# One product ahead of Down at the boundaries of the SwiGLU parts, product 3 last, fewer raw tiles at stage entries, and a layer norm in small steps

## The chip, the core and the metric

The kernel runs on one core of a Trainium2 chip. The metric is the device time of one execution in microseconds. The engines are named TensorE (PE; its weight loads are PEld), VectorE (DVE), ScalarE (ACT), GpSimd (POOL) and SyncE (SP); each runs its own queue in order and waits on semaphores of the others.

## The reference, cut to what matters

Two layers; x is 512 tokens by 1024 in float32. Each layer is two SwiGLUs with a mixer between them, each behind an RMS norm:

```
def swiglu(x, w_gate, w_up, w_down):
    return (jax.nn.silu(x @ w_gate) * (x @ w_up)) @ w_down
...
    for layer in range(DEPTH):
        x = x + 0.5 * swiglu(rms_norm(x, ffn_pre_norm[layer]), ffn_pre_w_gate[layer],
                             ffn_pre_w_up[layer], ffn_pre_w_down[layer])
        h = rms_norm(x, mix_norm[layer])
        if layer % 2 == 0:
            ...
            x = x + even_mixer(h, ...)
        else:
            ...
            x = x + odd_mixer(h, ...)
        x = x + 0.5 * swiglu(rms_norm(x, ffn_post_norm[layer]), ...)
    return rms_norm(x, final_norm)
```

The hidden width of a SwiGLU is 2816. The even mixer joins block-sparse attention with a gMLP: `u * (W_s LN(v) + b)` over chunks of 128 tokens, where LN is a layer norm over groups of 64 channels. The odd mixer is differential attention. Both end in an output projection.

## The kernel before, in words

All activations stay in SBUF, transposed: a tile is 128 channels by 512 tokens. Every product in float32 is made of three matmuls on split operands: each operand is rounded to a high part (`w_hi`, `xh`, `h`; the rounded type is called fp32r) and a low part, and hi·hi, lo·hi and hi·lo add up in one PSUM bank. Weights stream from HBM: SP issues the DMA of a raw tile, ScalarE makes `w_hi` from it (L127), VectorE makes `w_lo` by a subtraction (L128), and TensorE uses both. All three kinds of tile come from one pool of 14 buffers, `w4`.

`Stream` (L71 to L159) holds the program as a list of slots, each with the weight items that it needs and a function that emits its matmuls. When a slot is emitted, the items of the next three slots are split, and raw tiles further ahead are loaded, as many as the slot's number `raws` allows to be live. `st.later(n, fn)` puts a function n steps later. A scheduler makes every engine's queue out of these calls; the queues below are read from the built program.

A SwiGLU (`ffn`, L419) has 22 blocks of 128 hidden channels, 11 and their partners 11 further on. Block 0, 1 and their partners are done plainly (`first`, `gate`, `up`); the others in steps s of two partners by a Strassen–Winograd scheme of seven products in place of eight (`Seven`, L343; `Up`, L499). A product of a step is 24 matmuls of 128 by 256. Products 1, 6, 7 and 4 add up in bank A, product 2 in bank B, products 5 and 3 in bank D, and VectorE reads the banks between them:

```
    BANK = {1: "A", 6: "A", 7: "A", 4: "A", 2: "B", 5: "D", 3: "D"}
```

c11 (L543) reads B behind product 2, c22 (L556) reads D behind product 7 and before product 3 may write it, c12 (L566) reads D behind product 3, c21 (L579) reads A behind product 4. Products 5 and 6 take sums of weight quarters, which are made by an accumulating DMA on POOL (L359) and in `z` by VectorE (L369); product 3 takes `z` plus the quarter a12, which a second accumulating DMA loads once more (L384).

The steps are grouped in parts (steps 0 to 2, 3 to 5, 6 to 8, 9 to 10; `PARTS`, L417). The order within a step is 5, 6, 2, 7, product 1 of the next step, 3, 4 (L692). The last step of a part (`last(s)`) makes the operands of Down piecewise as soon as a quarter is there (`late`), so that Down can follow at once. Down multiplies the part's hidden blocks by their share of the down weights, again with seven products (`Down`, L591; 18 matmuls each), and its products stand in a list with the first products of the next part's step (L700): p and q are Down for the lower and upper pairs of output blocks, u the next step, v the one behind it. The last part is multiplied plainly (`down`, L615). Between SwiGLUs stand the mixers; `out_proj` (L709) works in chunks `begin` and `end`, and its `done` adds to x and feeds the norm of the SwiGLU that follows (`feed`, three operations on ScalarE and VectorE for each block). In `evac_gate` (L973) of the even mixer the gate is centred, and `finish_gate` (L994) makes the rsqrt for all four token blocks, scales and splits them at one step.

Of the kernel before, what the change touches and what calls it, by code (L numbers as in the profile page):

```python
# [15 lines left out]
OP = mybir.AluOpType  # L16
AX = mybir.AxisListType

P = 128
# [3 lines left out]
TT = T // P  # L23
# [9 lines left out]
def trunk_kernel(ctx: ExitStack, tc: tile.TileContext, a, out):  # L33
# [29 lines left out]
    class Item:  # L63
# [3 lines left out]
        def __init__(self, loads, raw, pre=None, frees=1, free_pre=0, ahead=0, post=None):  # L67
            self.loads, self.raw, self.pre, self.frees, self.free_pre = loads, raw, pre, frees, free_pre
            self.ahead, self.post = ahead, post
# [273 lines left out]
    class Seven:  # L343


        def __init__(self, n, dma):
            self.n, self.dma = n, dma
            self.raw, self.bank = {}, {}

        def load(self, name, *quarters):  # L350
# [11 lines left out]
        def item(self, c):  # L362
            r = self.raw

            def raw(n):
                return lambda: r[n]

            def add(dst, other):
                return lambda: nc.vector.tensor_add(r[dst], r[dst], r[other])  # L369

            if c == 1:
                return Item([self.load("a11", (0, 0))], raw("a11"), frees=0)
            if c == 2:
                return Item([self.load("a12", (0, 1))] if self.dma else [], raw("a12"))
            if c == 3:
                return Item([], raw("z")) if self.dma else Item([self.load("a12", (0, 1))], raw("z"), add("z", "a12"))
            if c == 4:
                return Item([self.load("a22", (1, 1))], raw("a22"))
            if c == 5:
                return Item([self.load("z", (1, 0), (1, 1))], raw("z"), frees=0, ahead=1)  # L380
            if c == 6:
                def post():
                    dst, s = self.source(r["z"], 0, 1)
                    nc.gpsimd.dma_start(dst, s, accum_op=OP.add)  # L384
                return Item([], raw("z"), add("z", "a11"), frees=0, free_pre=1, post=post if self.dma else None)
            return Item([self.load("c", (0, 0), (1, 0))], raw("c"), ahead=1)

        def slot(self, c):
# [30 lines left out]
    def ffn(which, norm, feed):  # L419
# [23 lines left out]
        def last(s):  # L443
            return any(s == e - 1 for _, e in PARTS)
# [54 lines left out]
        class Up(Seven):  # L499

            def __init__(self, s):
                super().__init__(4, True)
                self.s, self.seven = s, seven(s)
                self.late = last(s) and seven(s)
                self.v = {}
# [8 lines left out]
            def after(self, c):  # L514
                s = self.s
                if c in (1, 6):
                    return [(1, lambda: self.copied(c))]
                if c == 2:
                    return [(1, self.c11)]
                if c == 7:  # L520
                    return [(1, self.c22)]
                if c == 3:
                    if self.late:
                        return [(1, self.c12)]
                    return [(1, self.c12), (2, lambda: hidden(s))] + (
                        [] if self.seven else [(2 if last(s) else 3, lambda: whole_split(s))])
                if c == 4:
                    if self.late:
                        return [(1, self.c21)]
                    return [(1, self.c21), (1 if last(s) else 2, lambda: hidden(s + HF))] + (  # L530
                        [(2, lambda: first_operands(s)), (3, lambda: other_operands(s))] if self.seven
                        else [(1 if last(s) else 3, lambda: whole_split(s + HF))])
                return []

            def copied(self, c):
# [55 lines left out]
        class Down(Seven):  # L591

            def __init__(self, d, s0, s1):
                super().__init__(s1 - s0, False)
                self.d, self.s0, self.cols = d, s0, slice(s0 * P, s1 * P)

            def source(self, t, m, half):
# [54 lines left out]
        def first(wg, wu):  # L652
            norm.finish_soon(1 + int(which == 0))
            pg, pu = bank("pg"), bank("pu")
            for ks in [[k] for k in range(KT)] if which == 0 else (ORDER[:-1], ORDER[-1:]):
                for b, w in ((pg, wg), (pu, wu)):
                    project(b, w, norm, ks)
            for p in range(4):
                norm.whole(p)
            st.later(2 + int(which == 0), lambda: product(0, pg, pu))  # L660
            for p in range(4):
                st.later(1 + p, lambda p=p: norm.sums_for(p))

        def gate(f):
            def fn(w):
# [10 lines left out]
                    st.later(1, norm.last_sums)  # L676
            return fn

        def add(items, fn):
            st.add(items, fn, dense=True, raws=7)  # L680

        add([chunk(gu[0, 0]), chunk(gu[0, 1])], first)
        for f in range(plain):
            for f in (f, f + HF):
                if f > 0:
# [3 lines left out]
        steps[plain].add(1)  # L689
        for s0, s1 in PARTS:  # L690
            for s in range(max(s0, plain), s1):
                for c in (5, 6, 2, 7, 1, 3, 4):  # L692
                    if c == 1:
                        if s + 1 < HF and (s == plain or s > s0):
                            steps[s + 1].add(1)
                    elif s == plain or s > s0 or c in (3, 4):
                        steps[s].add(c)
            if s1 < HF:
                p, q, u, v = Down(0, s0, s1), Down(4, s0, s1), steps[s1], steps[s1 + 1]
                for o, c in ((p, 1), (u, 5), (u, 2), (p, 5), (u, 6), (p, 6), (p, 3), (u, 7), (p, 7), (p, 2),  # L700
                             (q, 1), (p, 4), (q, 5), (q, 6), (q, 3), (q, 7), (q, 2), (v, 1), (q, 4)):
                    o.add(c)
                continue
            cols = slice(s0 * P, s1 * P)
            for ds in [ORDER[:2]] + [(d,) for d in ORDER[2:]]:
                add([chunk(wd[0, d][:, cols], wd[1, d][:, cols]) for d in ds], down(ds, s0, s1))


    def out_proj(w, halves, hi, lo, feed):  # L709
        py = {}  # L710

        def mul(d, ws, ks):
            for k in ks:
                s = slice(((d % 2) * 4 + k % 4) * P, ((d % 2) * 4 + k % 4 + 1) * P)
                mm3(py[d], ws[0][:, s], ws[1][:, s], hi[k], lo[k],
                    k == halves[0][0], k == halves[1][-1])

        def done(d):
            nc.vector.tensor_add(x[d], py[d], x[d])
            feed(d)  # L720

        def begin(p):
            def fn(ws):
                for d in (2 * p, 2 * p + 1):
                    py[d] = bank("py")
                    mul(d, ws, halves[0])
            return fn

        def end(p):
            def fn(ws):  # L730
                for d in (2 * p, 2 * p + 1):
                    mul(d, ws, halves[1])
                    done(d)
            return fn

        def end_early(wa, wb):
            done_ks = {d: [] for d in range(4)}
            for k in halves[1]:
                for d in range(4):
                    if k in hi:  # L740
                        mul(d, (wa, wb)[d // 2], [k])
                        done_ks[d].append(k)
                st.step()
            st.drain()
            for d in range(4):
                mul(d, (wa, wb)[d // 2], [k for k in halves[1] if k not in done_ks[d]])
                done(d)

        st.add([chunk(w[0, 0])], begin(0))
        st.add([chunk(w[1, 0])], begin(1))  # L750
        st.add([chunk(w[2, 0])], begin(2))
        st.add([chunk(w[0, 1]), chunk(w[1, 1])], end_early)
        st.add([chunk(w[2, 1])], end(2), raws=7)
        st.add([chunk(w[3, 0])], begin(3), raws=7)
        st.add([chunk(w[3, 1])], end(3), raws=7)


    mask = const.tile([P, 512], F32, name="mask")
# [167 lines left out]
    def even_mixer(norm, feed):  # L926
# [46 lines left out]
        def evac_gate(b):  # L973
            gv = [two("gv") for _ in range(2)]
            for t in range(TT):
                g = gv[t // 2][:, t % 2]
                nc.scalar.activation(g, b[t], AF.Gelu_apprx_tanh, scale=norm.col[:, t:t + 1])
                cen[t] = g
            for t in range(TT):
                st.later(1 + t // 2, lambda t=t: center(t))  # L980
            st.later(3, finish_gate)

        def center(t):
            g = cen[t]
# [6 lines left out]
            nc.gpsimd.tensor_mul(sq, g, g)  # L991
            nc.vector.tensor_reduce(s2[:, t], by_group(sq), axis=AX.X, op=OP.add)

        def finish_gate():  # L994
            rsqrt(rs.rearrange("p t g -> p (t g)"), s2.rearrange("p t g -> p (t g)"), 1.0 / 64, TT * 8)
            for t in range(TT):
                g = cen[t]
                nc.vector.tensor_tensor(by_group(g), by_group(g),
                                        rs[:, t, :, None].to_broadcast([P, 8, 64]), op=OP.mult)
                split_gate(t)  # L1000

        def split_gate(t):
            gh[t], gl[t] = split(cen[t], "g", "h")
# [362 lines left out]
```

## Time and profile before

| | |
|---|---|
| three runs | 1874.03, 1874.51, 1879.26 us (median 1874.51) |
| the profiled execution | 1874.89 us, its span 1873.2 us |
| mean granted TensorE clock | 0.990 of full speed |
| busy | TensorE 1816.5, VectorE 1552.5, ScalarE 961.3, POOL 256.3 us |
| DMA | 288.25 MB in 153831 packets |

The page gives for each engine the time in which it executed something; idle time is put down to what ended it. A wait of TensorE on the path that sets the end costs its full length, and so does a stretch at a lower clock, which shows in the windows as a granted clock below 1.00. Idle time of the other engines costs nothing by itself. Sums below are made against the profiled execution, 1874.89 us, 0.38 us above the median.

### The profile page before, as it was taken

The numbers are of one execution on the slowest core, as the hardware profiler recorded it, in microseconds if no ns is written. First come the engines' busy times: TensorE is split into PE (matmuls) and PEld (weight loads), VectorE is DVE, ScalarE is ACT, GpSimd is POOL, SyncE is SP. The second block draws the span as 40 slices with busy tenths as digits, with TensorE's granted clock in tenths as the row PEclk, the third lists the DMA queues.
The fourth block names the chain that finished last, engine by engine and source line by source line (L and its number), as shares of the span: only waits on it lengthen the run. The fifth ranks groups of instructions, "written<-read, shape, count | busy, mean of one in ns | idle before, by whom it ended". The sixth has DMA issues, their size and how long they took to land. (4 is left out here: it accounts for less than half of the span.)

```text
span 1873.2 us, 32125 instructions
## 1 busy us (share of the span) xinstructions
PE 1816.5 (97%) x12624; PEld 1694.8 (90%) x12624; DVE 1552.5 (83%) x2515; ACT 961.3 (51%) x1523; POOL 256.3 (14%) x247
## 2 busy tenths in 40 slices
PE   7999999999999999999999999999999999999997
PEld 6999999878878999999899999988898789999996
DVE  7889898867957889897978989888889688888976
ACT  6545454533755545454644545464555454454544
POOL 0121111010410111111011212101111001111110
PEclk9999999999999999999999999999999999999999
DMA  7587877412334787876557878751223246878771
GB/s 225 128 218 178 213 177 190 148 61 75 97 106 113 156 225 162 232 162 172 167 121 183 208 188 205 189 156 57 91 80 91 102 116 141 217 163 217 172 193 61
DMA packets 153831, 288.25 MB, mean 154 GB/s; under 512 B 11840, under 2 KB 63696, under 8 KB 153680
## 3 DMA queue, kind: packets, MB, share of 16 engines
q1 hardware_dynamic: 110640, 209.62, 34.7%
q0 software_dynamic: 42464, 75.54, 24.7%
q8 instruction: 99, 1.62, 0.3%
q10 hardware_dynamic: 576, 1.05, 0.1%
q14 instruction: 52, 0.43, 0.1%
HBM read 277.77 MB, written 2.10 MB: 149 GB/s over the span
## 5 line engine op out<-in xcount | busy, mean ns | idle before, releaser
L127 ACT ACTIVATE w_hi<-w_raw 128x1024 fp32r<-128x1024 f32 (+2 forms) x542 | 517.8, 964 | 486.6 <-DVE w_raw L369 107.5
L128 DVE TENSOR_TENSOR w_lo<-w_raw,w_hi 128x1024 fp32r<-128x1024 f32 (+2 forms) x542 | 600.2, 1108 | 181.0 <-ACT w_hi L127 132.8
L359 POOL DMA_DIRECT2D w_raw<-in_gu x72 | 90.2, 1252 | 710.1 <-DMA w_raw<-in_gu 285.7
L402 PE MATMUL pA<-xt,w_hi 128*128 128x256 f32 x576 | 163.3, 284 | 0.7 <-ACT v L537 0.7
L402 PE MATMUL pA<-h,w_hi 128*128 128x256 f32 x576 | 163.0, 283 | 0.0
L403 PE MATMUL pA<-h,w_hi 128*128 128x256 f32 x576 | 163.0, 283 | 0.0
L404 PE MATMUL pA<-h,w_lo 128*128 128x256 f32 x576 | 163.0, 283 | 0.0
L404 PE MATMUL pA<-xt,w_lo 128*128 128x256 f32 x576 | 163.0, 283 | 0.0
L403 PE MATMUL pA<-xl,w_hi 128*128 128x256 f32 x576 | 163.0, 283 | 0.0
L403 PE MATMUL pA<-xt,w_hi 128*128 128x256 f32 x576 | 163.0, 283 | 0.0
L402 PE MATMUL pA<-xh,w_hi 128*128 128x256 f32 x576 | 163.0, 283 | 0.0
L404 PE MATMUL pA<-xh,w_lo 128*128 128x256 f32 x576 | 162.9, 283 | 0.0
L402 PEld LDWEIGHTS pA<-xt,w_hi 128*128 128x128 f32 x576 | 110.6, 192 | 1.0 <-ACT v L537 0.9
L403 PEld LDWEIGHTS pA<-xl,w_hi 128*128 128x128 f32 x576 | 110.6, 192 | 0.3
L402 PEld LDWEIGHTS pA<-xh,w_hi 128*128 128x128 f32 x576 | 110.6, 192 | 0.2
L402 PEld LDWEIGHTS pA<-h,w_hi 128*128 128x128 f32 x576 | 110.6, 192 | 0.0
L403 PEld LDWEIGHTS pA<-h,w_hi 128*128 128x128 f32 x576 | 110.6, 192 | 0.0
L404 PEld LDWEIGHTS pA<-h,w_lo 128*128 128x128 f32 x576 | 110.6, 192 | 0.0
L403 PEld LDWEIGHTS pA<-xt,w_hi 128*128 128x128 f32 x576 | 110.6, 192 | 0.0
L404 PEld LDWEIGHTS pA<-xh,w_lo 128*128 128x128 f32 x576 | 110.6, 192 | 0.0
L404 PEld LDWEIGHTS pA<-xt,w_lo 128*128 128x128 f32 x576 | 110.6, 192 | 0.0
L402 PE MATMUL pD<-h,w_hi 128*128 128x256 f32 x288 | 82.7, 287 | 9.9 <-ACT w_hi L127 9.9
(279 smaller groups left out, 5418.4 us busy)
## 6 DMA issues: line engine op xcount, KB each, us to landing
w_raw<-in_gu SPq DMA_DIRECT2D x210, 512.0 KB, 4.4
w_raw<-in_gu POOLq DMA_DIRECT2D x108, 512.0 KB, 6.1
w_raw<-in_wd SPq DMA_DIRECT2D x120, 384.0 KB, 3.6
w_raw<-in_wd POOLq DMA_DIRECT2D x48, 384.0 KB, 5.7
w_raw<-in_wd SPq DMA_DIRECT2D x64, 128.0 KB, 3.0
w_raw<-in_oqk SPq DMA_DIRECT2D x16, 512.0 KB, 4.6
ks<-ks SPq DMA_DIRECT2D x24, 256.0 KB, 3.4
w_raw<-in_eqk SPq DMA_DIRECT2D x8, 512.0 KB, 3.3
```

The source lines that it names most:

```text
L127: nc.scalar.activation(hi, raw, AF.Copy)
L128: nc.vector.tensor_sub(lo, raw, hi.bitcast(F32))
L359: nc.gpsimd.dma_start(dst, src, accum_op=OP.add)
L402: nc.tensor.matmul(o, w[0][:, s], t[0], start=new and p + j == 0, stop=False, **go)
L403: nc.tensor.matmul(o, w[0][:, s], t[1], start=False, stop=False, **go)
L404: nc.tensor.matmul(o, w[1][:, s], t[0], start=False, stop=p == self.n - 1, **go)
```

## The change

It has five parts. (1) At the boundary of two parts, product 6 of the next step stands ahead of Down's product 5. (2) In steps that are not the last of a part, product 4 stands ahead of product 3, and the work that followed product 4 follows product 3. In the last steps the order stays 3, 4, and `z` gets a12 there by an addition on VectorE, from a raw tile of a12 that is kept, in place of the accumulating DMA (16 of these DMAs fall away). (3) Fewer raw tiles may be live in the first slot of a SwiGLU (5, not 7) and in the last three of an output projection (4, 4 and 5, not 7). (4) In `first`, the sums of the norm's inputs come one step later. (5) In the gMLP's layer norm the rsqrt stands alone at its step, and the four token blocks are scaled and split at the two steps behind it, two at each.

```diff
@@ class Seven, item @@
             if c == 2:
-                return Item([self.load("a12", (0, 1))] if self.dma else [], raw("a12"))
+                known = self.order > 1
+                return Item([] if known else [self.load("a12", (0, 1))], raw("a12"), frees=int(known or self.order == 0))
             if c == 3:
-                return Item([], raw("z")) if self.dma else Item([self.load("a12", (0, 1))], raw("z"), add("z", "a12"))
+                if self.order == 0:
+                    return Item([], raw("z"))
+                known = self.order == 1
+                return Item([] if known else [self.load("a12", (0, 1))], raw("z"), add("z", "a12"), free_pre=int(known))
...
-                return Item([], raw("z"), add("z", "a11"), frees=0, free_pre=1, post=post if self.dma else None)
+                return Item([], raw("z"), add("z", "a11"), frees=0, free_pre=1, post=post if self.order == 0 else None)
@@ class Up, __init__ and after @@
-                super().__init__(4, True)
+                super().__init__(4, int(last(s)))
...
                 if c == 3:
                     if self.late:
                         return [(1, self.c12)]
+                    if last(s):
+                        return [(1, self.c12), (2, lambda: hidden(s)), (2, lambda: whole_split(s))]
                     return [(1, self.c12), (2, lambda: hidden(s))] + (
-                        [] if self.seven else [(2 if last(s) else 3, lambda: whole_split(s))])
+                        [(2, lambda: first_operands(s)), (3, lambda: other_operands(s))] if self.seven
+                        else [(3, lambda: whole_split(s))])
...
@@ class Down, __init__ @@
-                super().__init__(s1 - s0, False)
+                super().__init__(s1 - s0, 2)
@@ ffn @@
             for p in range(4):
-                st.later(1 + p, lambda p=p: norm.sums_for(p))
+                st.later(2 + p, lambda p=p: norm.sums_for(p))
...
-        add([chunk(gu[0, 0]), chunk(gu[0, 1])], first)
+        add([chunk(gu[0, 0]), chunk(gu[0, 1])], first, 5)
...
-                for c in (5, 6, 2, 7, 1, 3, 4):
+                for c in (5, 6, 2, 7, 1, 3, 4) if last(s) else (5, 6, 2, 7, 1, 4, 3):
...
-                for o, c in ((p, 1), (u, 5), (u, 2), (p, 5), (u, 6), (p, 6), (p, 3), (u, 7), (p, 7), (p, 2),
+                for o, c in ((p, 1), (u, 5), (u, 2), (u, 6), (p, 5), (p, 6), (p, 3), (u, 7), (p, 7), (p, 2),
@@ out_proj @@
-        st.add([chunk(w[2, 1])], end(2), raws=7)
-        st.add([chunk(w[3, 0])], begin(3), raws=7)
-        st.add([chunk(w[3, 1])], end(3), raws=7)
+        st.add([chunk(w[2, 1])], end(2), raws=4)
+        st.add([chunk(w[3, 0])], begin(3), raws=4)
+        st.add([chunk(w[3, 1])], end(3), raws=5)
@@ the gMLP's layer norm @@
             for t in range(TT):
                 st.later(1 + t // 2, lambda t=t: center(t))
-            st.later(3, finish_gate)
+                st.later(4 + t // 2, lambda t=t: finish_gate(t))
+            st.later(3, lambda: rsqrt(rs.rearrange("p t g -> p (t g)"), s2.rearrange("p t g -> p (t g)"),
+                                      1.0 / 64, TT * 8))
```

Three places of the engines' queues, before and in the change. The line numbers of the change are 4 or 8 higher for the same statements.

First TensorE at the first boundary of parts in the first SwiGLU: `pD<-xt` is product 5 of the next step, `pB` its product 2, `pD<-h` Down's product 5. Before:

```order
L404 MATMUL pD<-xt,w_lo 128x256
L402 MATMUL pB<-xh,w_hi 128x256
L403 MATMUL pB<-xl,w_hi 128x256
L402 MATMUL pD<-h,w_hi 128x256
L403 MATMUL pD<-h,w_hi 128x256
L404 MATMUL pB<-xh,w_lo 128x256
```

In the change:

```order
L408 MATMUL pD<-xt,w_lo 128x256
L406 MATMUL pB<-xh,w_hi 128x256
L407 MATMUL pB<-xl,w_hi 128x256
L408 MATMUL pB<-xh,w_lo 128x256
L406 MATMUL pB<-xh,w_hi 128x256
L407 MATMUL pB<-xl,w_hi 128x256
```

Down's first two matmuls of product 5 stood between the second and the third matmul of product 2; now all of product 2 stands in a row, product 6 behind it, and Down's product 5 behind that.

Next VectorE from the last operands of a middle step (step 4) to the reads of bank D in the last step of the second part (step 5): L545 and L553 are the same statement (c11), L560 and L568 of the change are c22, the L568 of before and L576 are c12. `w_lo_1854` belongs to product 3 (its raw tile is `z`), `w_lo_1895` to product 4. Before:

```order
L448 TENSOR_TENSOR h_1814<-h64_1810,h_1813 128x512
L545 TENSOR_TENSOR gu_1848<-v_1665,pB_1823 128x2x256
L128 TENSOR_TENSOR w_lo_1854<-w_raw_1360,w_hi_1853 128x1024
L547 TENSOR_TENSOR gu_1848<-gu_1848,R_374 128x2x256
L128 TENSOR_TENSOR w_lo_1895<-w_raw_1602,w_hi_1894 128x1024
L554 TENSOR_TENSOR gu_1848<-gu_1848 128x256
L560 TENSOR_TENSOR gu_1889<-v_1887,pD_1740 128x2x256
```

In the change:

```order
L584 TENSOR_TENSOR gu_1596<-gu_1596,R_358 128x1024
L128 TENSOR_TENSOR w_lo_1773<-w_raw_1451,w_hi_1772 128x1024
L445 TENSOR_TENSOR gu_1596<-gu_1596 128x512
L369 TENSOR_TENSOR w_raw_1360<-w_raw_1360,w_raw_1486 128x1024
L452 TENSOR_TENSOR h_1762<-gu_1596,h_1762 128x256
...
L562 TENSOR_TENSOR gu_1848<-gu_1848 128x256
L128 TENSOR_TENSOR w_lo_1854<-w_raw_1360,w_hi_1853 128x1024
L452 TENSOR_TENSOR h_1884<-gu_1848,h_1884 128x256
L568 TENSOR_TENSOR gu_1889<-v_1887,pD_1736 128x2x256
L128 TENSOR_TENSOR w_lo_1895<-w_raw_1602,w_hi_1894 128x1024
```

The row product of step 4 (L584) and the new sum of `z` (L369) now stand in this stretch, and the `w_lo` of product 4 has moved from ahead of c22 to behind it.

Last VectorE at the exit of the even mixer, where chunk `w_raw_5600` is the one of `begin(3)`. Before, its `w_lo` stands behind four feeds of the norm (L228, L238):

```order
L719 TENSOR_TENSOR x_70<-py_5482,x_70 128x512
L228 SCALAR_TENSOR_TENSOR xl_5820<-x_70,gains_71,xh_5819 128x512
L238 TENSOR_TENSOR acc_5823<-acc_5823,sq_5830 128x512
L228 SCALAR_TENSOR_TENSOR xl_5827<-x_70,gains_71,xh_5826 128x512
L238 TENSOR_TENSOR acc_5823<-acc_5823,sq_5838 128x512
L228 SCALAR_TENSOR_TENSOR xl_5835<-x_70,gains_71,xh_5834 128x512
L238 TENSOR_TENSOR acc_5823<-acc_5823,sq_5846 128x512
L228 SCALAR_TENSOR_TENSOR xl_5843<-x_70,gains_71,xh_5842 128x512
L128 TENSOR_TENSOR w_lo_5862<-w_raw_5600,w_hi_5861 128x1024
```

In the change it stands ahead of the last heads of the attention (L867, L1090 and L1076 are theirs):

```order
L128 TENSOR_TENSOR w_lo_5856<-w_raw_5600,w_hi_5855 128x1024
L1076 RECIPROCAL su_5648<-su_5648 128x4
L1090 TENSOR_TENSOR ml_5618<-o_5687,mh_5617 64x512
L867 TENSOR_TENSOR pl_5715<-pt_5700,ph_5713 128x512
L867 TENSOR_TENSOR pl_5719<-pt_5705,ph_5717 128x384
```

What stands behind the feeds of the norm there is now the `w_lo` of the last chunk, `end(3)`.

## Rows read from the trace of the kernel before

**Rows 1.** The page's part 1, engine by engine: busy us (share of the span) and the number of instructions.

```profile
PE 1816.5 (97%) x12624; PEld 1694.8 (90%) x12624; DVE 1552.5 (83%) x2515; ACT 961.3 (51%) x1523; POOL 256.3 (14%) x247
```

**Rows 2.** The table of waits of TensorE over the whole span: bank and line, what was waited for; then us in total, times, the longest in us.

```profile
PE pD L402 <- ACT w_hi L127: 9.9, 12, 0.8
PE pD L402 <- DVE gu L560: 7.9, 8, 2.9
...
PE py L179 <- DVE w_lo L128: 5.5, 2, 3.6
...
PE pu L177 <- ACT w_hi L127: 3.9, 1, 3.9
PE py L177 <- ACT w_hi L127: 2.6, 4, 0.7
...
PE pv L178 <- DVE w_lo L128: 1.7, 1, 1.7
PE pv L177 <- ACT w_hi L127: 1.3, 1, 1.3
```

**Rows 3.** The table of windows: the stretch in us, its length, then busy us (and instructions) of PE, PEld, DVE, ACT and POOL, the granted clock of TensorE as a share of full speed, the DMA share and GB/s. The first two stretches lie around the last steps of the first two parts of the first SwiGLU, the third in the layer norm of the even mixer, the fourth at the exit of the odd mixer.

```profile
72.00:90.00 18.00, 17.17 (x143) 16.97 (x142) 16.64 (x28) 9.84 (x18) 2.37 (x2) 1.00 0.67 143
165.00:183.00 18.00, 17.18 (x142) 16.86 (x141) 16.93 (x30) 10.34 (x18) 2.38 (x2) 1.00 0.62 135
409.00:417.00 8.00, 6.02 (x15) 4.43 (x16) 7.35 (x9) 5.87 (x8) 0.00 (x0) 0.60 0.37 129
1497.50:1506.00 8.50, 8.10 (x28) 6.51 (x29) 8.24 (x11) 5.45 (x7) 0.00 (x0) 0.80 0.18 62
```

**Rows 4.** TensorE's timeline at the first and the second boundary of parts (start us, us, engine, line, operation, out<-in; in brackets the idle time before it and what ended it; an operation's us hold its latency, so the steps are read from start to start).

```profile
88.61 0.28 PE L403 MATMUL pB<-xl,w_hi 128*128 128x256 f32 x1
89.72 0.39 PE L402 MATMUL pD<-h,w_hi 128*128 128x256 f32 x1 [0.83 <-ACT w_hi L127]
...
90.06 0.33 PE L404 MATMUL pB<-xh,w_lo 128*128 128x256 f32 x1
...
180.97 0.28 PE L402 MATMUL pB<-xh,w_hi 128*128 128x256 f32 x1
```

**Rows 5.** VectorE's timeline in front of the same two boundaries; of the 14 operations from 81.80 to 88.74, the first two and the last are shown, and the w_lo behind them.

```profile
81.80 0.68 DVE L568 TENSOR_TENSOR gu<-v,pD 128x512 f32<-128x512 f32 x1
82.39 1.22 DVE L369 TENSOR_TENSOR w_raw<-w_raw 128x1024 f32<-128x1024 f32 x1
...
88.40 0.42 DVE L448 TENSOR_TENSOR h<-h,h 128x256 fp32r<-128x256 f32 x1
88.74 1.22 DVE L128 TENSOR_TENSOR w_lo<-w_raw,w_hi 128x1024 fp32r<-128x1024 f32 x1
...
181.22 1.21 DVE L128 TENSOR_TENSOR w_lo<-w_raw,w_hi 128x1024 fp32r<-128x1024 f32 x1
```

**Rows 6.** ScalarE's timeline: the w_hi of u2 at the first boundary, and the w_hi of product 3 in a middle step.

```profile
86.82 1.04 ACT L127 ACTIVATE w_hi<-w_raw 128x1024 fp32r<-128x1024 f32 x1
...
144.43 1.06 ACT L127 ACTIVATE w_hi<-w_raw 128x1024 fp32r<-128x1024 f32 x1 [1.49 <-DMA w_raw<-in_gu]
```

**Rows 7.** Operations around bank D: VectorE's read at c22 in the last step of the second part, TensorE's first matmul of product 3 behind it, and the first two of product 3 in a middle step.

```profile
169.34 0.68 DVE L560 TENSOR_TENSOR gu<-v,pD 128x512 f32<-128x512 f32 x1
...
170.08 0.39 PE L402 MATMUL pD<-xh,w_hi 128*128 128x256 f32 x1
...
243.19 0.39 PE L402 MATMUL pD<-xh,w_hi 128*128 128x256 f32 x1 [1.18 <-DVE gu L560]
243.41 0.28 PE L403 MATMUL pD<-xl,w_hi 128*128 128x256 f32 x1
```

**Rows 8.** TensorE's timeline in the layer norm of the even mixer; the matmuls between are alike.

```profile
409.24 0.73 PE L177 MATMUL pv<-w_hi,xh 128*128 128x512 f32 x2 [1.29 <-ACT w_hi L127]
411.71 0.79 PE L178 MATMUL pv<-w_lo,xh 128*128 128x512 f32 x1 [1.74 <-DVE w_lo L128]
...
417.40 0.39 PE L177 MATMUL pv<-w_hi,xh 128*128 128x512 f32 x1
```

**Rows 9.** VectorE's timeline there: the first operation of the rsqrt, and the gate products behind its last (an x3 is three operations of the kind in a row, their times together).

```profile
403.38 0.18 DVE L201 TENSOR_SCALAR rs<-ln_s 128x32 f32<-128x32 f32 x1
...
405.62 1.89 DVE L998 TENSOR_TENSOR gv<-gv,ln_rs 128x512 f32<-128x512 f32 x3
```

**Rows 10.** TensorE's timeline at the exits of the even and of the odd mixer.

```profile
557.08 0.62 PE L179 MATMUL py<-mh,w_lo 128*128 128x512 f32 x1 [1.96 <-DVE w_lo L128]
...
560.83 0.40 PE L179 MATMUL py<-m,w_lo 128*128 128x512 f32 x1
...
1497.90 0.50 PE L179 MATMUL py<-m,w_lo 128*128 128x512 f32 x1 [3.56 <-DVE w_lo L128]
```

**Rows 11.** ScalarE at the entry of the first SwiGLU.

```profile
28.85 1.04 ACT L127 ACTIVATE w_hi<-w_raw 128x1024 fp32r<-128x1024 f32 x1
```

**Rows 12.** ScalarE at the end of the first SwiGLU.

```profile
327.93 1.06 ACT L127 ACTIVATE w_hi<-w_raw 128x1024 fp32r<-128x1024 f32 x1 [1.82 <-DMA w_raw<-in_gu]
```

**Rows 13.** The entry of the second SwiGLU: ScalarE's w_hi, VectorE's last operation of the norm's rsqrt, and TensorE's transposes of its column.

```profile
579.21 1.06 ACT L127 ACTIVATE w_hi<-w_raw 128x1024 fp32r<-128x1024 f32 x1 [1.57 <-PE pg L179]
...
584.29 0.15 DVE L212 SCALAR_TENSOR_TENSOR rcol<-rs,rs 128x4 f32<-128x4 f32 x1
...
586.09 0.38 PE L315 MATMUL pr<-ident,rcol 128*128 128x128 f32 x2
```

More of the change, by code (lines that the diff above doesn't have):

```diff
@@ L343, in trunk_kernel, with __init__ @@
     class Seven:
-        def __init__(self, n, dma):
-            self.n, self.dma = n, dma
+        def __init__(self, n, order):
+            self.n, self.order = n, order
             self.raw, self.bank = {}, {}
@@ L529, in after @@
                         return [(1, self.c21)]
-                    return [(1, self.c21), (1 if last(s) else 2, lambda: hidden(s + HF))] + (
-                        [(2, lambda: first_operands(s)), (3, lambda: other_operands(s))] if self.seven
-                        else [(1 if last(s) else 3, lambda: whole_split(s + HF))])
+                    if last(s):
+                        return [(1, self.c21), (1, lambda: hidden(s + HF)), (1, lambda: whole_split(s + HF))]
+                    return [(1, self.c21), (2, lambda: hidden(s + HF))] + (
+                        [] if self.seven else [(3, lambda: whole_split(s + HF))])
                 return []
@@ L677, in up, with add @@
             return fn
-        def add(items, fn):
-            st.add(items, fn, dense=True, raws=7)
-        add([chunk(gu[0, 0]), chunk(gu[0, 1])], first)
+        def add(items, fn, raws=7):
+            st.add(items, fn, dense=True, raws=raws)
+        add([chunk(gu[0, 0]), chunk(gu[0, 1])], first, 5)
         for f in range(plain):
@@ L992, in center, with finish_gate @@
             nc.vector.tensor_reduce(s2[:, t], by_group(sq), axis=AX.X, op=OP.add)
[L994 to L1000, printed above, removed]
+        def finish_gate(t):
+            g = cen[t]
+            nc.vector.tensor_tensor(by_group(g), by_group(g),
+                                    rs[:, t, :, None].to_broadcast([P, 8, 64]), op=OP.mult)
+            split_gate(t)
         def split_gate(t):
```

## The prediction

> **What bounds the kernel now.** I read the page's busy times first. TensorE is busy 97% of the 1873.2 us span, so whatever is won must come out of about 57 us in which it is idle, plus the stretches in which it runs at half rate [rows 1]. The table of TensorE's waits shows where that idle time lies: not in one place, but in a dozen waits of 0.8 us and eight of 1 us, both at recurring places of the SwiGLUs, and in a few single waits of 1.3 to 3.9 us at the entries and exits of stages [rows 2]. Then I read the timelines of these places on TensorE and on the engine named, and the table of windows for the granted clock. The windows also show the other limit: in the last steps of a part VectorE is busy 16.64 and 16.93 of 18 us [rows 3]. Every step that needs something from VectorE there gets it when its in-order queue has come to it.
>
> **Boundary of two parts, 12 times.** TensorE does two matmuls of product 2 of the next step (u2), then two of Down's product 5, which wait 0.83 us for an operand and ScalarE's w_hi, and only then u2's third matmul, which uses w_lo [rows 4]. From 88.61 to 90.06 three matmul steps (of 0.12 us each) take 1.45 us in place of 0.36 us: 1.09 us lost. The new order puts all of u2 and u6 in front of p5. But the third matmul of u2 needs w_lo, and that subtraction ran 88.74 to 89.96; at the second boundary 181.22 to 182.43, with u2 started at 180.97 [rows 4, 5]. VectorE gets there through 14 instructions without idle time from the read of product 3 at 81.80 [rows 5], and the order of VectorE's queue between these two is the same in the change, except that the z sum stands a little later. So I take the wait to stay, as a wait of u2 for VectorE's w_lo: the third matmul would start at about 90.06 and not at 88.73, 1.33 us lost, 0.24 us more than now. Behind parts 1 and 2 one more subtraction of 0.34 us (88.40 to 88.74 is one such step [rows 5]) stands behind product 3's read, so 0.58 us more. 4 x 0.24 + 8 x 0.58 = **+5.6 us**. Bounds: 12 x 1.09 = 13.1 us gained if VectorE is in time; 12 x (0.24 + 1.22) = 17.5 us lost if one more operation of 1.22 us stands in its way each time.
>
> **Middle steps, 8 times.** Product 3 waits for c22, VectorE's read of bank D, 7.9 us in all [rows 2]. Behind it stands ScalarE's w_hi, held 1.49 us in one of them by the accumulating DMA [rows 6], and everything on VectorE slides with it; in another product 3 waits 1.18 us, until 243.19 [rows 7]. With product 4 first, c22 has 2.9 us more and the wait goes: 7.9 us and 8 x 0.1 us of slow pick-up (0.22 us to the second matmul [rows 7]), −8.7 us. In the last step of parts 1 and 2 product 3 stays where it was, with no slack now: c22 ends at 170.02, product 3 starts at 170.08 [rows 7]. Ahead of this c22 the new queue has two more operations of 1.22 us (the z sum, the row product), and one of 0.34 us more, and less: the w_lo of product 4, 1.22 us, and one product of 0.60 us. Net 0.96 us, of which some goes into idle time (VectorE is busy 16.93 of 18 us there [rows 3]): 0.75 us x 8 = +6.0 us. Together **−2.7 us**; bounds −8.7 (all absorbed) and +6 (the waits of the middle steps are replaced by others as long, and the new one at the last steps is 1.5 us).
>
> The DMA that goes is issued by POOL, which is 14% busy, and it frees nothing that TensorE waits for elsewhere. Raw a12 is kept one slot longer; the next raw tile is asked for later, but SP's tiles are ready well ahead of ScalarE except at the accumulating ones [rows 6]. I cost both at nothing.
>
> **Layer norm, once.** TensorE waits 1.29 us for w_hi, which ScalarE makes behind three gh copies, then 1.74 us for w_lo, behind gate products [rows 8]. From 411.71 to 417.40 it does 14 matmul steps at 0.427 us; at 0.225 us that is 3.15, so 2.5 us more [rows 8], and the window shows the granted clock at 0.60 [rows 3]: most of it at the lower of its two levels, 1.2 and not 2.4 GHz. Now w_hi stands ahead of gh, and w_lo behind two gate products only: 403.4 + 2.24 (the rsqrt, to 405.62) + 2 x 0.6 and 0.6 (two gate products and one of the u, a third of 1.89 each [rows 9]) + 1.22 (w_lo, as in [rows 5]) = 408.7, where TensorE would want it at 409.24 − 1.29 + 2 x 0.225 = 408.4; with the pick-up 0.5 us left. 1.29 + 1.74 + 2.5 − 0.5 = **−5.0 us**. The Trainium skill ("TensorE: Matmul & The Clock Gate", "What's actually happening") says that the clock is low by default, that activity lifts it, and that the chip judges by a grid of its own, so that the number of slow matmuls varies between runs. By that the 2.5 us could come back at another wait; the sum would then be 2.5 us higher. The row of 243.19, a wait of 1.18 us with matmuls of 0.12 us right behind [rows 7], speaks against it for a wait of 0.5 us. Bounds −2.5 and −5.5.
>
> **Exits of the mixers, twice.** TensorE waits 1.96 us (557.08) and 3.56 us (1497.90) for w_lo of the last chunk but one, whose subtraction stands behind four feeds of the norm on VectorE [rows 10]. Half rate adds 557.08 to 560.83 − 9 x 0.225 = 1.7 us, and as much in the second, where the clock is 0.80 over 8.5 us [rows 3]. In the new order that chunk is split before the last heads, and only the chunk behind it waits in that queue. Of 1.96 + 3.56 + 2 x 1.7 = 8.9 us I take **−8.0 us**, since VectorE's feeds, now earlier by 1.22 us, leave the last chunk's w_lo little room. Bounds −8.9 and +1.
>
> **Entry of the first SwiGLU, and ends of the four.** w_hi of the up chunk runs 28.85 to 29.89 behind ScalarE's norm sums, TensorE waits 3.9 us [rows 2, 11]. sums_for one step later moves it four operations of 0.4 us ahead, but its wait is then for the raw tile: **−1.2 us** (−4 to +1). At the four ends of a SwiGLU py waits 2.6 us in all for ScalarE's w_hi [rows 2], behind a w_hi held 1.82 us by the DMA that goes [rows 12]; a VectorE sum takes its place, as long as the 1.22 us of [rows 5]: **−1.2 us** of the 2.6 (−2.6 to 0).
>
> **Sum.** 5.6 − 2.7 − 5.0 − 8.0 − 1.2 − 1.2 = −12.5 us. The profiled execution took 1874.89 us (the span and 1.7 us), so 1862.4; the median of the runs stands 0.4 us below the profiled one: **1862.0 us**. All lower bounds together would be 1831, all upper ones 1897; neither is likely as a whole.
>
> **Rivals.**
> 1. *VectorE is in time* (chance 0.13). Then the waits at the boundaries and the middle steps go whole: −13.1 − 8.7 − 15.4 = −37.2 us, **1837 us**. For it: w_hi of u2 is done at 87.86 [rows 6], 0.88 us before VectorE takes up w_lo. Against it: the gapless queue of [rows 5].
> 2. *The entries only move their wait* (0.15). Fewer raw tiles make ScalarE's w_hi wait for TensorE's release (one waited 1.57 us until 579.21), and the row of the norm, made from the rsqrt's column, comes late to the SwiGLU [rows 13]. The two exits then give nothing and the entry loses 1: 1862.0 + 8.0 + 2.2 = **1872 us**, no change. Against it: the column ends at 584.44 and its transposes start at 586.09, 1.65 us to spare [rows 13], and the two w_lo that stood around its start stand ahead of the norm's sums now.
> 3. *VectorE becomes the bound, slower* (0.07). The 16 z sums of 1.22 us are new on it, 19.5 us. If a last step has no idle time left, each lies on the path: +19.5 in place of my 6.0 us, and the boundaries at their upper bound, +17.5 in place of 5.6: 1862.0 + 13.5 + 11.9 = **1887 us**. It decides from 18.1 us on (1880.1 − 1862.0), 0.65 us more than I took at each of the 16 z sums and 12 boundaries. The Trainium skill ("Perfetto Trace Analysis", "Optimizing Scalar/DVE Operations") advises to move work off VectorE where it is saturated; this change moves work onto it. The trace bears that out only for the last steps (94% busy [rows 3]), not for the kernel (83% [rows 1]), hence the small chance.
>
> **How the numbers follow.** My forecast has 0.65. A measurement of this kernel tells 0.3%, 5.6 us, from no change: faster is below 1868.9, slower above 1880.1. Of the 0.65, 0.03 falls above 1868.9. Faster 0.62 + 0.13 = 0.75, same 0.03 + 0.15 = 0.18, slower 0.07. The range, 1850 to 1873, takes in the forecast's bounds (−12 when half of the boundaries' wait goes) and rival 2; rivals 1 and 3 lie outside.
>
> **What the changed profile would show.** Right: the waits "pD for w_hi" (9.9 us) and "pD for gu of c22" (7.9 us) are gone or much shorter; in their place pB for VectorE's w_lo, 12 times, 1.2 to 1.8 us, and pD for gu of c22 in 8 last steps, below 1 us; no wait above 0.7 us at the layer norm and no clock of 0.60 there; py for w_lo of 5.5 us gone. Wrong: no wait of pB for w_lo (then rival 1), new waits of pr or pg at the second and fourth SwiGLU (rival 2), VectorE above 95% in the last steps with waits of 1.5 us behind it (rival 3), or a half-rate stretch behind the boundaries.

## The result, and the profile after

The changed kernel takes 1856.83 us (median of 4 runs, 1855.80 to 1857.99) against 1874.27 us before (4 runs, 1871.28 to 1879.26). The ratio is 0.9904, with a 95% interval of 0.9882 to 0.9927: faster by 17.4 us, where 12.5 was forecast. The forecast of 1862.0 us with the range 1850 to 1873 holds; the terms behind it hold less well, and two large misses cancel.

The changed kernel's table of TensorE's waits answers to [rows 2] (engine, bank and line, what was waited for: us in total, times, longest):

```profile
PE pB L408 <- DVE w_lo L128: 17.2, 12, 1.6
PE pg L177 <- ACT xh L227: 5.7, 1, 5.7
PE pr L315 <- DVE ocol L212: 3.3, 2, 3.1
PE py L177 <- ACT w_hi L127: 2.3, 4, 0.6
PE pr L315 <- DVE lcol L212: 2.0, 1, 2.0
PE pu L177 <- ACT w_hi L127: 1.3, 1, 1.3
...
PE pv L178 <- DVE w_lo L128: 0.5, 1, 0.5
```

The waits of pD for w_hi (9.9 us) and for c22's gu (7.9 us) have no row any more, nor has py for w_lo (5.5 us). In place of the first stands pB for w_lo, 12 times, as forecast (1.2 to 1.8 us each), 17.2 us in all where the wait that it replaces had 9.9. pv has 0.5 us left, the figure of the forecast.

The table of windows at the places of [rows 3], moved to where they lie now, and the entry of the first SwiGLU as the last (columns as there):

```profile
72.00:90.00 18.00, 16.88 (x141) 16.68 (x140) 16.42 (x28) 8.24 (x15) 3.55 (x3) 1.00 0.59 120
161.00:179.00 18.00, 16.41 (x133) 15.85 (x133) 17.44 (x31) 10.15 (x18) 2.38 (x2) 1.00 0.72 163
405.00:413.00 8.00, 7.47 (x33) 5.85 (x32) 8.00 (x11) 6.04 (x9) 0.00 (x0) 1.00 0.23 73
1480.00:1488.50 8.50, 8.50 (x39) 6.98 (x39) 8.42 (x14) 6.36 (x11) 0.00 (x0) 1.00 0.36 125
26.00:38.00 12.00, 10.61 (x48) 8.28 (x47) 12.00 (x22) 9.54 (x16) 1.19 (x1) 1.00 0.78 178
```

The granted clock is 1.00 in the layer norm (0.60 before) and at the exit of the odd mixer (0.80), and 33 and 39 matmuls pass in the same length where 15 and 28 did. In the last step of the second part VectorE is now busy 17.44 of 18 us (97%). The forecast had named more than 95% there, with waits of 1.5 us behind it, as a sign of its third rival; that sign has come, and the time of that rival has not.

At the entry of the first SwiGLU the granted clock was below 1.00 before; this row of the kernel before belongs to the last one above:

```profile
26.00:38.00 12.00, 8.05 (x25) 5.96 (x25) 9.12 (x21) 6.03 (x10) 1.19 (x1) 0.72 0.80 176
```

To compare place by place, the time lost was summed from the trace: for each matmul the time to the next start, less columns / 2.4 GHz and 12 ns, so that waits, slow pick-up and half rate all count.

| Place | Forecast | Lost before | Lost after | Measured |
|---|---|---|---|---|
| 12 boundaries | +5.6 | 15.6 | 30.1 | +14.5 |
| 8 stretches between two boundaries (middle and last steps) | −2.7 | 19.2 | 8.5 | −10.7 |
| layer norm | −5.0 | 6.4 | 1.1 | −5.3 |
| two exits | −8.0 | 10.0 | 0.6 | −9.3 |
| entry of the first SwiGLU | −1.2 | 7.1 | 2.2 | −4.9 |
| four ends of a SwiGLU | −1.2 | 5.0 | 3.8 | −1.2 |
| sum | −12.5 | | | −16.9 |

The sum agrees with the spans, 1873.2 and 1856.3 us.

The boundaries show why the first line is so large. TensorE's timeline at the second boundary (start us, us, engine, line, operation, out<-in, and in brackets the idle time before it with what ended it) answers to [rows 4]:

```profile
176.55 0.39 PE L406 MATMUL pB<-xh,w_hi 128*128 128x256 f32 x1
176.77 0.28 PE L407 MATMUL pB<-xl,w_hi 128*128 128x256 f32 x1
178.64 0.39 PE L408 MATMUL pB<-xh,w_lo 128*128 128x256 f32 x1 [1.59 <-DVE w_lo L128]
...
179.34 0.28 PE L407 MATMUL pB<-xl,w_hi 128*128 128x256 f32 x1
179.46 0.32 PE L408 MATMUL pB<-xh,w_lo 128*128 128x256 f32 x1
179.58 0.41 PE L406 MATMUL pB<-xh,w_hi 128*128 128x256 f32 x1
179.79 0.41 PE L407 MATMUL pB<-xl,w_hi 128*128 128x256 f32 x1
180.00 0.41 PE L408 MATMUL pB<-xh,w_lo 128*128 128x256 f32 x1
```

The wait is 1.59 us, and about 0.9 us after it the steps go from 0.12 to 0.21 us, for 16 matmuls. At the third boundary the steps stay at 0.12 us behind the same wait:

```profile
273.15 0.39 PE L408 MATMUL pB<-xh,w_lo 128*128 128x256 f32 x1 [1.59 <-DVE w_lo L128]
...
274.33 0.28 PE L408 MATMUL pB<-xh,w_lo 128*128 128x256 f32 x1
274.45 0.28 PE L406 MATMUL pB<-xh,w_hi 128*128 128x256 f32 x1
```

The windows around the two places show the granted clock at 0.57 and at 1.00:

```profile
179.00:183.00 4.00, 4.00 (x24) 4.00 (x23) 1.92 (x2) 0.24 (x1) 1.19 (x1) 0.57 0.20 22
271.00:275.00 4.00, 2.41 (x18) 2.15 (x18) 4.00 (x7) 2.41 (x5) 0.00 (x0) 1.00 0.20 73
```

Four boundaries, the first of each SwiGLU, lose 1.53 us. Of the other eight, the second and third of each, four lose 2.26 us and four, with the half-rate stretch, 3.73 us. Before, all twelve lost 1.30 us. "Parts 1 and 2", in the prediction and below, counts the parts from 0: these eight boundaries are the ones behind them.

### The profile page after: what moved, and what is told of

It reads as the page before. It is cut to its first block, busy times and chain, and to the rows that moved or that the text cites. A ratio compares the mean times of both kernels' runs of the same rounds, so it can differ in the third digit from the quotient of the medians.

```text
span 1856.3 us, 32166 instructions
## 1 busy us (share of the span) xinstructions
PE 1812.4 (98%) x12624; PEld 1694.4 (91%) x12624; DVE 1565.8 (84%) x2531; ACT 957.3 (52%) x1523; POOL 236.8 (13%) x231
## 5 line engine op out<-in xcount | busy, mean ns | idle before, releaser
L369 DVE TENSOR_TENSOR w_raw<-w_raw 128x1024 f32<-128x1024 f32 (+1 forms) x100 | 109.3, 1093 | 1.5
```

## The experiments

The kernel before was run beside them on each chip; its medians there were 1872.6, 1872.3 and 1870.2 us. Behind each time stand its ratio to that kernel and, in brackets, the 95% interval of the ratio. The runs stand on different chips, so a difference between two of them is also given by their ratios where it matters. What is lost "at the boundaries" is the sum of the table's first line.

**The parts apart.** The change without its first part, and the kernel before with the first part alone, each by this line (shown for the former):

```diff
-                for o, c in ((p, 1), (u, 5), (u, 2), (u, 6), (p, 5), (p, 6), ...
+                for o, c in ((p, 1), (u, 5), (u, 2), (p, 5), (u, 6), (p, 6), ...
```

> The change with its first part undone (Down's product 5 again ahead of the next step's product 6). Theory: this part is a loss. In the changed kernel TensorE waits 17.2 us for w_lo at the 12 boundaries, where it waited 9.9 us, and behind some of these waits about 14 matmuls run at half rate (0.215 us a step); undone, the waits are again about 0.83 us each and the half-rate stretches go: 12 us less, 1845 us (1842 to 1849). Rival: the wait is VectorE's lag alone, whatever stands on TensorE; the order only gives it another name, and the time stays within 3 us of 1857 us.

Measured: 1847.92 us, 0.987 (0.985 to 0.9891), 8.9 us faster than the whole change (6.4 by the ratios). The boundaries lose 21.4 us (1.30 at four, 2.02 at eight) and not 30.1, and no half-rate stretch follows them. The rival falls; the first part is a loss, of 6 to 9 and not of 12 us.

> The kernel before with the first part alone. Theory: 12 waits of pB for w_lo of 1.2 to 1.3 us in place of 12 of 0.83 us, 5 to 12 us more than before, about 1883 us. Rival: VectorE's lag comes from the new z sums, so without them w_lo is in time and the wait goes: 1862 us.

Measured: 1876.11 us, 1.0023 (1.0007 to 1.0039). All twelve boundaries lose 1.54 us, 18.4 in all:

```profile
PE pB L404 <- DVE w_lo L128: 13.4, 12, 1.1
```

That is 0.24 us more each, as the forecast's first step had it, and no half-rate stretch. The whole is 3.5 us (4.3 by the ratio), a little less than the 5 to 12 us expected. The rival falls: VectorE is late without the z sums too.

The second part alone (the change with the other four undone):

> The kernel before with the second part alone: product 4 ahead of product 3 in all but last steps, the z sum on VectorE in last steps. Theory: the 8 waits of product 3 go whole (8.7 us) and the new wait of the last steps does not come, because c22 is still in time: 1865 us. Rival (the term as predicted): 0.75 us more at each of 8 last steps, 1871 us.

Measured: 1865.89 us, 0.9966 (0.9953 to 0.9978). The wait of product 3 has no row, but the boundaries of parts 1 and 2 lose 2.02 us where they lost 1.30, with the old order of the boundary, too: 0.72 us at 8 places, 5.8 us, given back. The new wait of the last steps does not come, and its rival falls with it.

The third to fifth parts alone (the edits of the diff to `out_proj`, `first`, its sums and the layer norm, on the kernel before):

> The kernel before with the third, fourth and fifth parts alone: fewer raw tiles at the entries, the sums one step later, the layer norm in small steps. Theory: 5.8 us from the layer norm, 9.2 us from the two exits, 5 us from the entry of the first SwiGLU, half of each a wait and half its half-rate stretch: 1854 us. Rival: part of it is only moved to later waits (pr, pg at the entries), 1862 us or more.

Measured: 1855.78 us, 0.9916 (0.9895 to 0.9936): 16.8 us, though product 3's waits, 7.9 us before, came to 11.9 us in this run:

```profile
PE pD L402 <- DVE gu L560: 11.9, 8, 3.2
PE pD L402 <- ACT w_hi L127: 9.9, 12, 0.8
```

No new wait stands at the entries. The three pieces, +3.5, −6.7 and −16.8 us, come to −20.0 where the whole brought 17.4; by the ratios they come to −17.8 against 18.0, so times alone do not tell the pieces' sum from the whole. The traces of the boundaries do: 2.8 and 5.8 us more are lost in the two pieces, and 14.5 us in the whole. The 5.9 us between are four half-rate stretches of 1.47 us, which neither wait (1.1 us with the new order alone, 1.3 us with the second part alone) brought with it.

**What makes VectorE late.** The changed kernel with the z sums of the last steps back on the DMA:

```diff
-                super().__init__(4, int(last(s)))
+                super().__init__(4, 0)
```

> The changed kernel with the z of the last steps again completed by the accumulating DMA and not by VectorE; all else as changed. Theory: the z sum is what pushes VectorE's queue back behind product 3 in the last steps of parts 1 and 2; without it the 8 boundary losses of 2.26 us and more become the 1.54 us of the others, no half-rate stretch follows, 11 us less: 1846 us. Rival: the lag at these boundaries comes from the later operands of Down alone, the time stays at 1857 us, or rises where the DMA holds w_hi again.

Measured: 1855.14 us, 0.9918 (0.9895 to 0.9942), the time of the change. The boundaries lose 29.0 us, 1.54 at four, about 2.3 or 3.8 at eight. The theory's 11 us do not come. The run does not clear the z sum, though, because the wait has changed:

```profile
PE pB L408 <- DVE w_lo L128: 10.9, 12, 1.1
PE pB L406 <- ACT w_hi L127: 6.4, 8, 0.8
```

At the eight places TensorE waits less for VectorE's w_lo, and 0.8 us for ScalarE's w_hi of u2 instead. In VectorE's queue the `w_lo` of product 4 stands ahead of c22 again here, as in the kernel before; u2's w_lo ends 12.63 us after the first matmul of product 3, against 12.96 in the change and 12.36 before. So a part of VectorE's lag went, and another wait took its place.

Then the queue in front of u2's w_lo was made shorter. Product 5 of the next step before Down's product 1, on the old order of the boundary, puts the update of x behind w_lo:

```diff
-                for o, c in ((p, 1), (u, 5), (u, 2), (u, 6), (p, 5), (p, 6), ...
+                for o, c in ((u, 5), (p, 1), (u, 2), (p, 5), (u, 6), (p, 6), ...
```

> The change with its boundary order undone and only the swap of product 5 and Down's product 1, so that the update of x (0.60 us) stands behind u2's w_lo; the z sum stays on VectorE. Theory: 0.60 us less at each of 12 boundaries, 7 us below 1847.9: 1841 us. Rival (ScalarE's w_hi or h is what is late): 1848 us.

Measured: 1836.57 us, 0.9817 (0.9794 to 0.9839), 20 us below the change (16 by the ratios) and 11.4 below the run without the swap (10 by the ratios). The boundaries lose 9.2 us, 0.48 at four and 0.92 at eight, which is 0.82 and 1.10 us less than without the swap, and not 0.60. At the second boundary VectorE's queue has no pause any more, its read of product 3 starts 3.17 us after that product's first matmul and not 4.59, and Down's w_lo (0.87 us) falls behind that read: 0.60 + 1.42 − 0.87 = 1.15 us, and u2's w_lo ends 1.13 us earlier there. The swap did more than move the update of x. The wait that is left:

```profile
PE pB L408 <- DVE w_lo L128: 3.9, 8, 0.5
```

The same swap with the new order of the boundary:

> The changed kernel, boundary order as changed, with product 5 of the next step ahead of Down's product 1. Theory: at the same lag of VectorE the new order loses about 0.24 us more than the old one, whatever the lag is, so 0.7 us at 4 and 1.2 us at 8 boundaries, 12 us in all where the old order with this swap lost 9.2: 1839 to 1843 us. Rival: with the lag below 1 us the new order hides it: 4 us or less lost, about 1830 us.

Measured: 1837.50 us, 0.9823 (0.9787 to 0.9860). The boundaries lose 11.2 us, 0.49 at four and 1.15 at eight. Where a wait is left the new order costs 0.23 us more, where none is left it costs nothing; in time the two orders can't be told apart. The theory's time was 1.5 us or more too high, and the rival, that the order hides the lag, falls.

Down's product 5 ahead of u2 as well, `((u, 5), (p, 1), (p, 5), (u, 2), (u, 6), (p, 6), ...`:

> The change with the boundary order product 5 of the next step, Down's 1, Down's 5, then products 2 and 6 of the next step. Theory: what ends the wait is the w_lo of the first product that needs a late one; Down's is of 768 columns and takes 0.95 and not 1.22 us, and 2.1 us of its matmuls cover u2's: 0.3 us less at each of 12 boundaries than the 1836.6 us of the swap alone, 1833 us. Rival: Down's product 5 waits for its h, made by ScalarE and VectorE behind the same queue: 1837 us or more.

Measured: 1836.50 us, 0.9816 (0.9773 to 0.9860), no different from the swap alone; the boundaries lose 9.2 us in both. pD waits for its w_lo in place of pB, 3.7 us at 8 places, and not for h, as the rival had it. The theory's 0.3 us a boundary did not come.

Last, the sum for z of product 6 in the first step behind each boundary was moved from VectorE to GpSimd, on top of the swap, with the old and with the new order:

```diff
+                pre = add("z", "a11")
+                if getattr(self, "s", 0) in (3, 6, 9):
+                    pre = lambda: nc.gpsimd.tensor_add(r["z"], r["z"], r["a11"])
-                return Item([], raw("z"), add("z", "a11"), ...
+                return Item([], raw("z"), pre, ...
```

> The change with its boundary order undone, and VectorE's queue in front of u2's w_lo made shorter in two ways: the sum that gives product 6 of a part's first step its z runs on GpSimd (1.14 us a place off VectorE), and product 5 of that step stands ahead of Down's product 1, so that the update of x (0.60 us) falls behind w_lo. Theory (VectorE's lag is the whole of the boundary wait): the 1.30 us lost at 4 and 2.02 us at 8 boundaries fall by up to 1.74 us each, to 0 and 0.3, 19 us less than the 1847.9 us of the change without its boundary part: 1829 us. Rival (the wait hangs on ScalarE's w_hi, or GpSimd's addition slows VectorE): 1840 us or more, with waits of about 1 us left.

> The same two moves on the changed kernel, boundary order as changed. Theory: with w_lo in time the new order does what it says, no matmul of the boundary waits, and the 30.1 us lost at the 12 boundaries fall to 2 or 3 us, half-rate stretches gone with the waits: 1857 − 27 = 1830 us, the same as or a little below the run with the old order. Rival: waits of 1 us stay, 1845 us.

Measured: 1877.85 us, 1.0034 (1.0022 to 1.0046), and 1880.08 us, 1.0040 (1.0025 to 1.0055), 41 and 43 us slower than the swap without it. In the former the boundaries lose 49.7 us. VectorE's and GpSimd's timelines at its second boundary show what happens, the rival's second half:

```profile
171.70 0.69 DVE L579 TENSOR_TENSOR gu<-v,pD 128x512 f32<-128x512 f32 x1
172.30 2.98 DVE L455 TENSOR_TENSOR h<-gu,h 128x256 fp32r<-128x256 f32 x1
175.21 0.68 DVE L581 TENSOR_TENSOR gu<-gu,R 128x512 f32<-128x512 f32 x1
```

```profile
172.11 2.88 POOL L391 TENSOR_TENSOR w_raw<-w_raw 128x1024 f32<-128x1024 f32 x1
```

A subtraction that takes 0.42 us elsewhere takes 2.98 us, until GpSimd's addition ends at 174.99; at 11 of the 12 places one takes 2.97 to 3.72 us. The Trainium skill ("SBUF — State Buffer", "SBUF: two separate sides") says that the two engines share a pair of ports, which an instruction of GpSimd holds to its end while one of VectorE with two SBUF inputs waits; the rows agree. So the 1.14 us taken off VectorE came back as 2.56 us on it. The net, about 1.42 us at 12 places, makes 17 of the 41 us, and half-rate steps around the boundaries make 13 more; the rest was not followed up.

**The entry of the first SwiGLU.** Seven raw tiles again in the first slot, and, apart from it, the sums a step earlier again:

```diff
-        add([chunk(gu[0, 0]), chunk(gu[0, 1])], first, 5)
+        add([chunk(gu[0, 0]), chunk(gu[0, 1])], first)
```

> The changed kernel with seven raw tiles again in the first slot of a SwiGLU (all else as changed). Theory: the fewer raw tiles are what moved ScalarE's w_hi of the first up chunk ahead of four of the norm's sums; undone, TensorE waits 3.9 us there again and runs 12 us at a clock of about 0.72: 5 us more, 1862 us. Rival: it was the step of the sums: no change there.

Measured, one run with a profile: 1859.01 us. The wait is back, and with it a granted clock of 0.72:

```profile
PE pu L177 <- ACT w_hi L127: 4.3, 1, 4.3
...
26.00:38.00 12.00, 7.80 (x22) 5.86 (x23) 9.25 (x19) 6.49 (x12) 1.74 (x2) 0.72 0.82 178
```

> The changed kernel with the sums of the norm's inputs a step earlier again. Theory: the wait at the first SwiGLU's entry stays near 1.3 us; the sums' step is not what moved w_hi. Rival: the wait is 3.9 us again, and the time 5 us more.

Measured, one run with a profile: 1855.45 us, and pu waits 0.8 us. The wait tells it, since one time each does not: the raw tiles made the gain, the step of the sums none.

## Why the prediction was right, and where it was not

**Boundary.** The mechanism was right: the wait stays under another name, because the third matmul of u2 needs VectorE's w_lo. The term was mis-sized, +5.6 against +14.5 us. Of it, 0.24 us for each of 12 was exact (the new order alone). The 0.34 us for the boundaries behind parts 1 and 2 was 0.72 us. VectorE's queue at the second boundary shows 0.60 of it; before:

```profile
171.87 0.42 DVE L554 TENSOR_TENSOR gu<-gu 128x256 f32<-128x256 f32 x1
172.77 0.43 DVE L448 TENSOR_TENSOR h<-gu,h 128x256 fp32r<-128x256 f32 x1 [0.48 <-ACT h L447]
173.13 1.23 DVE L128 TENSOR_TENSOR w_lo<-w_raw,w_hi 128x1024 fp32r<-128x1024 f32 x1
174.28 0.68 DVE L568 TENSOR_TENSOR gu<-v,pD 128x512 f32<-128x512 f32 x1
```

In the change:

```profile
168.74 1.23 DVE L128 TENSOR_TENSOR w_lo<-w_raw,w_hi 128x1024 fp32r<-128x1024 f32 x1 [0.56 <-issue]
169.88 0.42 DVE L562 TENSOR_TENSOR gu<-gu 128x256 f32<-128x256 f32 x1
170.21 0.68 DVE L576 TENSOR_TENSOR gu<-v,pD 128x512 f32<-128x512 f32 x1
170.81 0.42 DVE L452 TENSOR_TENSOR h<-gu,h 128x256 fp32r<-128x256 f32 x1
```

The w_lo shown is that of product 5 of the next step; it starts 3.05 and 3.11 us after the first matmul of product 3. Two operations that follow c22, a step of 0.34 us each (L554 and L448, now L562 and L452), stood ahead of it and stand behind it now, and u2's w_lo ends 12.96 us after that matmul and not 12.36. I counted one of the two. What moved them goes back to the next step of my working, which lets the `w_lo` of product 4 out behind c22, ahead of them; that is read from the queues and was not tried by itself. The remaining 0.12 us was not followed up. And I carried no term for the clock: the text named a half-rate stretch as a sign of a wrong forecast, and it came behind four waits of 1.59 us, 5.9 us in all.

**Middle and last steps.** −2.7 against −10.7 us. The 8.7 us of product 3's waits went as forecast, and 2.0 us more with them, of which 1.1 us is a half-rate stretch of 12 matmuls that had stood behind the longest of these waits. The +6.0 us set against it, a new wait for c22 in the last steps, did not come: VectorE's read of bank D (L568) and the first matmul behind it are as close as before [rows 7]:

```profile
164.89 0.68 DVE L568 TENSOR_TENSOR gu<-v,pD 128x512 f32<-128x512 f32 x1
```

```profile
165.39 0.28 PE L406 MATMUL pA<-xh,w_hi 128*128 128x256 f32 x1
165.63 0.39 PE L406 MATMUL pD<-xh,w_hi 128*128 128x256 f32 x1
```

The step that failed is the net of 0.96 us, put against an engine with 1 us of idle time in 18: no wait came of it. VectorE's timeline shows no wait from 151.40 to 168.18 here, and then 0.56 us of idle time, at all eight places, so the added operations of 1.22 us are done by then; the profile names no releaser of that pause, which ends as TensorE ends product 3 (168.76). What I let be paid at c22 was paid behind it, and not as a lag that is carried over, but by the order of the queue: two operations behind the pause. The two steps of the working, 0.34 us at the boundary and 0.75 us at c22, became 0.72 us at the boundary, and the clock added 1.47 us at four of the eight.

**Layer norm.** −5.0 against −5.3 us, 0.53 us of wait left against 0.5. The half-rate stretch did not come back; the granted clock is 1.00. The rule of the Trainium skill that I weighed there ("TensorE: Matmul & The Clock Gate", "What's actually happening") showed itself elsewhere: of eight equal waits at the boundaries four are followed by a stretch at the lower level and four are not, which agrees with a chip that judges on a grid of its own. In the two runs on the entry, with waits of 1.6 us at the same eight places, it is three of eight each time, and not the same three.

**Exits.** −8.0 against −9.3 us; I kept 0.9 us for the last chunk's w_lo, which was in time. **Entry of the first SwiGLU.** −1.2 against −4.9 us: I moved w_hi by its four operations and did not follow the half-rate stretch behind the wait, which went with it, though [rows 2] and the layer norm showed the pattern. **Ends.** −1.2 against −1.2 us.

**Rivals.** "VectorE is in time" fell at the boundaries (17.2 us of waits) and held at c22. "The entries only move their wait" fell: pr and pg have no new row at the second and fourth SwiGLU. "VectorE becomes the bound" fell in time, but not in its signs: VectorE is busy 97% in the last step shown, waits of 1.59 us stand behind it, and VectorE's queue is what the losses at the boundaries hang on.

## What to carry to other kernels

A product put in front of a late operand helps only if its own operands are there: look up the last operand of the first instruction that moves up, and when its engine gets to it. When an operation is moved in a full queue, follow what it pushes back, operation by operation, to the next place that waits for that queue. What paid here was to change what stands in the queue's stretch ahead of that place, as the swap of two products did (16 to 20 us below the change), and not the order of the products that wait. A forecast whose total is right can hold two large terms that are wrong: here +8.9 and −8.0 us cancelled, and that was luck.

## What the runs showed of the hardware that was not expected

A GpSimd addition of 128 x 1024 in float32 took 2.88 us and held up a VectorE subtraction of 128 x 256 for 2.56 us, from 0.42 to 2.98 us. Behind waits of TensorE of 1.59 us, 16 matmuls each ran at the clock's lower level (0.21 and not 0.12 us a step) at four of eight places in one run and at three of eight in two others; behind waits of 1.1 us at twelve places, and of 1.3 us at eight, none did.
